# Input projection of a hybrid layer as seven products of 2x2 blocks, with its results taken through DRAM

## The chip, the cores and the metric

The kernel runs on one core of a Trainium2 chip. The metric is the device time of one execution in microseconds. The engines of the core are TensorE (PE in the profile; its weight loads are PEld), VectorE (DVE), ScalarE (ACT), GpSimd (POOL) and SyncE (SP), which issues nearly all DMAs of this kernel from one queue.

## What is computed

One layer of a decoder on 1024 prompt tokens and 64 sample tokens (8 sequences of 8), width 1024, float32: an FFN, a token mixing, a second FFN, and a final norm. The mixing projects each normed token to 8224 columns, and mixes by two branches:

```python
proj = hn @ w_in                                  # 1024 -> 1024 u, 2048 z, 3072 xbc, 32 dt, 2 x 1024 gates
branch_pool = pool_mix(u_ext, ...) @ pool_w_out   # trailing means over 2, 4, 8, 16 tokens, minus the token
xbc_c = silu(depthwise causal conv of width 4 over xbc)
dt = softplus(dt_raw + dt_bias)
y, new_ssm = ssd_scan(xs, dt, A, bm, cm, ssm_h0)  # Mamba-2 scan in chunks of 128 tokens, 32 heads in 4 groups
y = (y + d_skip * xs) * silu(z)                   # then an RMSNorm within each of the 4 groups
branch_ssd = y @ ssd_w_out
merged = sigmoid(g0) * branch_pool + sigmoid(g1) * branch_ssd
x = x + merged @ w_o
```

The last rows of u and xbc and the scan's states are outputs as well.

## The kernel before

**Layout.** Activations lie with channels on the 128 partitions and tokens along the free dimension. The tokens are worked on in two halves: half 0 has 512 prompt tokens, half 1 the other 512 and the 64 sample tokens, 576 in all. Matmul operands are kept as a high and a low part (F32R), and a product of two such operands is three matmuls: `products` (L274) issues high x high, high x low, low x high. `load_w` (L261) brings 4 blocks of 128 x 128 weights (256 KB), and ScalarE (L270) and VectorE (L271) split them into `wh` and `wl`. `dense` (L285) makes a tile of 128 output columns from 1024 input rows: 8 blocks x 3 matmuls of 512 columns for half 0, and twice as many of 288 for half 1.

**Seven products.** The FFNs make their first product for both halves at once by `wino` (L441): the matrix of weights is taken as 2x2 blocks of 512 rows x 128 columns, the tokens of a half as two quarters of 256 or 288, and seven products with sums of blocks replace eight. `wino_weights` (L402) forms the sums of weights on GpSimd (L411) and splits them (L417, L418); `combine` (L459) forms the sums of the operands on GpSimd (L472) and splits them (L478, L479); the results are added up when they leave PSUM. While `combine` works, the first tiles of an FFN are made by the plain form.

**The order.** The program is written out in full by Python, and its order decides what each engine finds next. Work that goes on beside the large products is a generator, a "chain" (`start`, `later`); `pe[0]` counts the TensorE time written so far, each chain says in how many microseconds of it the next step is due, and `tick`, called after each block of products, lets due chains write their step. `finish` writes all the rest of one chain at once. The pool of DMAs on SP's queue follows the same order.

**The mixing stage, half by half** (`mix_half`, L1260). It makes dt (`mix_dt`, L769), then u tile by tile with its trailing means, the group maps, the gates of the first branch and `pool_w_out` (`mix_pool`, L853), whose merged result goes to DRAM (`accd`). Then the four groups of the scan follow: `proj_group` (L985) makes a group's 6 conv tiles (`conv_tile`, L955: product, copy, four taps on ScalarE and VectorE, a tanh and a last product for SiLU). While the products of the next group and the z tiles (`z_tiles`, L1266) are written, the chain `ssd_group` (L1208) does the scan of the present one: for each chunk `ssd_a` (L1059) loads the broadcast decay rows (`ab`), transposes x, forms the masked decays and the operands; `ssd_b` (L1119) makes y and `ssd_st` (L1187) the next state. The y products (L1175 to L1180) use a zero-padded operand `xdtp`, 128 columns for two heads of 64, so that two matmuls add up into one block. For half 1 a fifth step per group does the sample tokens with their own states from DRAM. `gating` (L1240) multiplies by z, takes the group's norm (`rstd`, L325: squares, a column sum on TensorE, Newton steps on VectorE, a round trip through DRAM to spread the result over the partitions) and splits; then `ssd_out` (L1277) makes the group's part of `ssd_w_out`. In the last group the tiles of the second gate (`gate1`, L1288) are written, four of them between the scan and the wait for the last norm; then come the merge (`merge_head`, L1320) and `w_o`. Half 1 is normed (`norm_split`, L366) while half 0 is in `w_o`.

`N_ACT = 58` buffers of 128 x 576 are shared by most tiles of the stage.

Of the kernel before, what the change touches and what calls it, by code (L numbers as in the profile page):

```python
# [14 lines left out]
P = 128  # L15
# [22 lines left out]
N_FX, N_S, N_PDF = 17, 4, 6  # L38
N_PLAIN, N_APART = 3, 1
# [5 lines left out]
CONV_D = (1.0, 3.0)  # L45
# [12 lines left out]
N_PRE = 3  # L58


@with_exitstack
def tile_hybrid_pool_ssd_macaron(
# [42 lines left out]
    def fx(dt=F32, name="x"):  # L105
        if stage["name"] == "mix":
            return act((P, 576), dt, name)
        return stage["p"].tile([P, 576], dt, tag="fx", bufs=N_FX, name=nm(name))
# [101 lines left out]
    cwh = cp.tile([P, 5, 24], F32, tag="cwh", name="cwh")  # L210
# [10 lines left out]
    xdt_n = [0]  # L221
# [4 lines left out]
    def load_consts():  # L226
# [17 lines left out]
        for j in range(4):  # L244
            V.tensor_scalar_mul(cwh[:, j, :], cols[:, i_cw[j] : i_cw[j] + 24], 0.5)
        V.tensor_scalar_mul(cwh[:, 4, :], cols[:, i_cb : i_cb + 24], 0.5)
# [5 lines left out]
    accd = [[dp.tile([P, NTOK[h]], F32, tag=f"ac{h}_{m}", name=f"accd{h}_{m}") for m in range(KD)] for h in HALVES]  # L252
    acs_d = [dp.tile([4, NH, CH], F32, tag=f"acsd{h}", name=f"acsd{h}") for h in HALVES]
# [71 lines left out]
    def rstd(tiles, h, count, out, pace=1.0):  # L325
# [3 lines left out]
        s = act((P, N), name="ssq")  # L329
        for i, x in enumerate(tiles):  # L330
            if i == 0:
                S.activation(s, x, AF.Square)
            else:
                q = act((P, N), name="sq")
                S.activation(q, x, AF.Square)
                V.tensor_tensor(s, s, q, op=ALU.add)
            if i % 2:
                yield pace
# [26 lines left out]

    def norm_split(xt, h, gi, out, pace=1.0):  # L366

        N = NTOK[h]
        rr = []
        yield from rstd(xt, h, D, rr, pace)  # L370
        hi, lo = [], []
        for k in range(KD):
            a = act((P, N), F32R, "hi")
            b = act((P, N), F32R, "lo")
            t = act((P, N), name="xn")
            V.tensor_tensor(t, xt[k], rr[0], op=ALU.mult)
            split(t, a, b, cols[:, gi + k : gi + k + 1])
            hi.append(a)
            lo.append(b)
            yield pace  # L380
        out.append((h, hi, lo))

    def scaled(out, pts, h, r):

        for pt, (a, b) in zip(pts, PIECES[h]):
            V.tensor_tensor(out[:, a:b], pt[:, : b - a], r[:, a:b], op=ALU.mult)
# [162 lines left out]
    def ffn(wi, wo, prep, after, half=None):  # L549

        X, todo, behind = [{}, {}], [], []
        for h in HALVES:
# [10 lines left out]
            c = start(first(gen), T_AT[h + (2 if half else 0)])  # L565
            for ff in range(N_PLAIN):
                ffn_in_plain(wi, ff, x[:3])
            todo.append(c)
            behind.append(start(rest(c, gen)))
        for c in behind:  # L570
            finish(c)
        for ff in range(N_PLAIN, NFF - N_APART):
            ffn_in(wi, ff, [(h, X[h]) for h in HALVES])
# [3 lines left out]
        for h in HALVES:  # L577
# [12 lines left out]
            for ms in ((0, 1),) + tuple((m,) for m in range(2, KD)):  # L590
# [8 lines left out]
                for m, pts in zip(ms, po):  # L599
# [4 lines left out]
                    xt.append(x_)  # L604
                if half and ms[-1] == KD // 2 - 1:
                    half(h, xt)
# [87 lines left out]
    def norm_parts(xt, h, gi, out, pace=1.0):  # L694
# [3 lines left out]
        yield from rstd([t[:, :N] for t in xt], h, D, rr, pace)  # L698
        hi, lo, xn = [], [], []
        for k in range(KD):  # L700
            x = fx(name="xn") if k >= 4 else act((P, 576), name="xn")
            a, b = act((P, 576), F32R, "hi"), act((P, 576), F32R, "lo")
            V.scalar_tensor_tensor(x[:, :N], xt[k][:, :N], cols[:, gi + k : gi + k + 1], rr[0], op0=ALU.mult, op1=ALU.mult)
            split(x[:, :N], a[:, :N], b[:, :N])
            hi.append(a)
# [6 lines left out]
    ch, hn = {}, []  # L712
    wi1 = ffn1_w_in[0]

    def after1(h, xt):
        if h == 0:
            ch["hn"] = start(norm_split([t[:, : NTOK[0]] for t in xt], 0, i_gm, hn, HN_PACE))
        for m in range(KD):
            dma(xspill[h][m], xt[m][:, : NTOK[h]])
# [17 lines left out]
    ffn(wi1, ffn1_w_out[0], prep1, after1)  # L737
    finish(ch["hn"])
# [4 lines left out]
    xdtp = [stage["p"].tile([P, 4, 2, P], F32, tag=f"xdtp{i}", bufs=1, name=f"xdtp{i}") for i in range(2)]  # L743
    for t in xdtp:
        G.memset(t, 0.0)
    W = w_in[0]
    uhist = cp.tile([P, KD, HIST], F32, tag="uhist", name="uhist")
    chist = cp.tile([P, 24, 3], F32, tag="chist", name="chist")
# [11 lines left out]
    def evac_raw(pts, h, raw, off, raws, offs):  # L760

        if h == 0:
            S.copy(raw[:, off : off + 512], pts[0][:, :512])
            return
        S.copy(raw[:, off : off + 288], pts[0][:, :288])  # L765
        S.copy(raw[:, off + 288 : off + 512], pts[1][:, :224])
        S.copy(raws[:, :, offs : offs + NT], pts[1][:, 224:288].rearrange("p (b t) -> p b t", t=NT))

    def mix_dt(h, xs, out):  # L769
# [4 lines left out]
        pd = dense(W, 0, KD, OFF_DT, xs, name="pdt")[0]  # L774
        dfm = act((NH, N), name="dfm")
        for pt, (a, b) in zip(pd, PIECES[h]):
            S.activation(dfm[:, a:b], pt[:NH, : b - a], AF.Identity, bias=dtb)

        def chain():
            yield 8  # L780
# [28 lines left out]
            yield 12  # L809
# [40 lines left out]

        return start(chain())

    def mix_pool(h, xs, sin):  # L853

        N = NTOK[h]
        if h == 1:
# [71 lines left out]
        for gi in range(4):  # L928
            u_tile(2 * gi)
            u_tile(2 * gi + 1)  # L930
            if gi:
                group(gi - 1)
# [564 lines left out]
```

## Time and profile before

| | |
|---|---|
| median of 3 runs | 3033.59 us (3032.02 to 3039.48) |
| the profiled execution, first to last instruction | 3038.7 us |
| mean granted TensorE clock | 0.991 |
| TensorE busy | 2948.8 us, 97% |
| VectorE busy | 1747.2 us, 57% |
| ScalarE busy | 1263.1 us, 42% |
| GpSimd busy | 408.0 us, 13% |
| moved by DMA | 352.09 MB, 116 GB/s on average |

The page gives no time for the profiled execution beside its span. Durations below come from it alone. "Busy" of an engine is the time in which at least one of its instructions runs; matmuls are pipelined and their ends are modelled, so what one costs is read from start to start.

### The profile page before, as it was taken

To read this page: it belongs to the slowest core of one execution; us is meant where nothing else is said; L and a number is where in the kernel's file an instruction comes from. 1 tells how busy PE (TensorE), PEld (TensorE's weight loads), DVE (VectorE), ACT (ScalarE), POOL (GpSimd) and SP (SyncE) were. 2 spreads that over 40 slices of the span, in tenths; PEclk is the share of its full clock that TensorE was granted. 3 is DMA by queue.
4 is the path that set the end of the run, shared out by engine and by line. 5 is a ranking of instruction groups with operands and counts; after the bars stand their busy time and mean duration, and the time that the engine had idled before them with its cause. 6 is when DMAs were issued, how large, how long until landed. Compare 5 with 4: busy or idle time off the path is not lost. (4 is left out here: it accounts for less than half of the span.)

```text
span 3038.7 us, 51391 instructions
## 1 busy us (share of the span) xinstructions
PE 2948.8 (97%) x19636; PEld 2746.9 (90%) x19636; DVE 1747.2 (57%) x3456; ACT 1263.1 (42%) x2552; POOL 408.0 (13%) x491
## 2 busy tenths in 40 slices
PE   6999999999999999999999999999998999999998
PEld 5999999789988888878999989999988999997898
DVE  5544345434364897777725886968776433344442
ACT  5343334433243665434424554543344333343332
POOL 4333333000000000000001110100014333330000
PEclk9999999999999999999999999999999999999999
DMA  4443223653334333345333334244452222225552
GB/s 127 143 126 99 72 79 106 219 165 114 103 101 121 108 105 101 101 122 174 97 102 100 111 104 128 89 138 125 130 159 85 86 71 79 76 92 174 162 168 72
DMA packets 519273, 352.09 MB, mean 116 GB/s; under 512 B 27162, under 2 KB 460432, under 8 KB 519018
## 3 DMA queue, kind: packets, MB, share of 16 engines
q1 hardware_dynamic: 519010, 348.80, 38.4%
q8 instruction: 154, 2.52, 0.3%
q14 instruction: 93, 0.76, 0.1%
q10 hardware_dynamic: 16, 0.00, 0.0%
HBM read 291.65 MB, written 57.29 MB: 115 GB/s over the span
## 5 line engine op out<-in xcount | busy, mean ns | idle before, releaser
L270 ACT ACTIVATE wh<-wraw 128x512 fp32r<-128x512 f32 (+1 forms) x636 | 391.2, 619 | 806.2 <-PE po L160 257.7
L271 DVE TENSOR_TENSOR wl<-wraw,wh 128x512 fp32r<-128x512 f32 (+1 forms) x636 | 436.2, 688 | 494.3 <-ACT wh L270 466.7
L160 PE MATMUL pw<-hi,wh 128*128 128x288 f32 (+1 forms) x1216 | 351.7, 289 | 2.6 <-DVE t L522 2.2
L160 PE MATMUL pw<-hi,wl 128*128 128x288 f32 (+1 forms) x1216 | 350.8, 288 | 0.0
L160 PE MATMUL pw<-lo,wh 128*128 128x288 f32 (+1 forms) x1216 | 350.5, 288 | 0.0
L160 PE MATMUL pw<-X,wh 128*128 128x288 f32 (+1 forms) x1824 | 347.3, 289 | 1.1 <-ACT t L518 1.1
L160 PE MATMUL po<-hh,wh 128*128 128x288 f32 (+1 forms) x1056 | 289.7, 332 | 11.1 <-ACT hh L308 10.1
L160 PE MATMUL po<-hr,wh 128*128 128x288 f32 (+1 forms) x1056 | 290.3, 330 | 0.5 <-DVE hr L310 0.2
L160 PE MATMUL po<-hh,wl 128*128 128x288 f32 (+1 forms) x1056 | 289.8, 329 | 0.0
L160 PEld LDWEIGHTS pw<-X,wh 128*128 128x128 f32 x1824 | 288.1, 190 | 1.4 <-ACT t L518 1.4
L160 PE MATMUL pw<-X,wl 128*128 128x288 f32 (+1 forms) x912 | 263.0, 288 | 0.0
L160 PEld LDWEIGHTS pw<-hi,wh 128*128 128x128 f32 x1216 | 230.2, 189 | 3.5 <-DVE t L522 2.6
L160 PEld LDWEIGHTS pw<-lo,wh 128*128 128x128 f32 x1216 | 230.2, 189 | 0.0
L160 PEld LDWEIGHTS pw<-hi,wl 128*128 128x128 f32 x1216 | 230.1, 189 | 0.0
L418 DVE TENSOR_TENSOR wl<-s,wh 128x512 fp32r<-128x512 f32 x160 | 114.0, 714 | 175.3 <-ACT wh L417 172.5
L160 PEld LDWEIGHTS po<-hh,wh 128*128 128x128 f32 x1056 | 179.8, 190 | 30.2 <-ACT hh L308 15.3
L160 PEld LDWEIGHTS po<-hr,wh 128*128 128x128 f32 x1056 | 181.0, 190 | 17.5 <-DVE hr L310 3.9
L160 PEld LDWEIGHTS po<-hh,wl 128*128 128x128 f32 x1056 | 181.0, 190 | 14.6 <-DVE wl L271 0.7
L417 ACT ACTIVATE wh<-s 128x512 fp32r<-128x512 f32 x160 | 101.1, 632 | 181.4 <-PE pw L160 180.1
L160 PEld LDWEIGHTS pw<-X,wl 128*128 128x128 f32 x912 | 173.6, 190 | 0.0
L160 PE MATMUL pc<-hi,wh 128*128 128x288 f32 (+1 forms) x576 | 162.3, 335 | 0.7 <-ACT craw L765 0.6
L160 PE MATMUL pc<-hi,wl 128*128 128x288 f32 (+1 forms) x576 | 159.8, 329 | 0.3 <-DVE wl L271 0.3
(345 smaller groups left out, 6470.0 us busy)
## 6 DMA issues: line engine op xcount, KB each, us to landing
wraw<-in_w_in_dram SPq DMA_DIRECT2D x260, 256.0 KB
wraw<-in_ffn_w_in_dram SPq DMA_DIRECT2D x208, 256.0 KB
wraw<-in_ffn_w_out_dram SPq DMA_DIRECT2D x160, 256.0 KB
ab<-acsd SPq DMA_DIRECT2D x64, 256.0 KB
wraw<-in_ssd_w_out_dram SPq DMA_DIRECT2D x64, 256.0 KB
hd<-g SPq DMA_DIRECT2D x44, 288.0 KB
hr<-hd SPq DMA_DIRECT2D x44, 288.0 KB
hd<-g SPq DMA_DIRECT2D x44, 256.0 KB
```

The lines of the kernel that those rows point to most:

```text
L160: T.matmul(out, lhsT, rhs, start=start, stop=stop, skip_group_check=free)
L270: S.activation(wh, raw, AF.Copy)
L271: V.tensor_tensor(wl, raw, wh.bitcast(F32), op=ALU.subtract)
L417: S.activation(wh, a, AF.Copy)
L418: V.tensor_tensor(wl, a, wh.bitcast(F32), op=ALU.subtract)
```

## The change

**A projection stage of its own.** After the first FFN, still with its buffers and its 6 + 2 PSUM banks, all of the projection is made for both halves. dt and the first four z tiles are made plainly, half by half (`plain_in`), while the operands are combined; the other 60 tiles are made in pairs by `wino` (`proj_pair`). The trailing means and the convolution follow as chains on VectorE and ScalarE. SiLU is now one ScalarE function, where tanh and a product stood. All results go to DRAM: `convd`, `zd`, `gd`, `ddd`, `dtd_`. The squares for the norm between are taken as the FFN's tiles are finished (`squares`), and the normed half 0 is kept in DRAM (`xnd`) until it is combined.

**The mixing stage** loads these half by half. The scan of all 8 units (2 halves x 4 groups) is one chain, which may run `AHEAD = 2` groups in front of `ssd_out`. `mix_pool` of both halves stands first, then `mix_out` of half 0 and of half 1, each with `ssd_out` group by group, the merge and `w_o`.

**The y products** lose their zero padding: each head's 64 columns go to their own 64 partitions of the result. Four kinds of operation move from VectorE to GpSimd: the product with z, the last sum of y, the decay of the state, and one sum of the merge.

```diff
-N_FX, N_S, N_PDF = 17, 4, 6
-N_PLAIN, N_APART = 3, 1
+N_FX, N_S, N_PDF = 16, 4, 6
+N_PLAIN, N_APART, N_ZP = 3, 1, 4
...
+    def proj_pair(ca, cb, off, done, halves=HALVES, weights=None):
+        xs = [(h, XM[h]) for h in halves]
+        tiles = {}
+
+        def after(p, i, bk):
...
+            if p == "1":
+                S.copy(rb[:, l], A)
+            elif p == "2":
+                V.tensor_tensor(ra[:, f], B, rb[:, l], op=ALU.add)
+            elif p == "6":
+                S.copy(rb[:, f], A)
+            elif p == "5":
+                S.copy(rb[:, l], C)
+            elif p == "7":
+                V.tensor_tensor(rb[:, l], A, rb[:, l], op=ALU.add)
+            elif p == "3":
+                V.tensor_tensor(ra[:, l], C, rb[:, f], op=ALU.add)
+            else:
+                S.copy(rb[:, f], A)
+                done(h, ra, rb)
+
+        wino(wino_weights(W, 0, 4, 4, ca, cb), 4, xs, after)
...
+    def whole(f, scale, da, db):
+        def done(h, ra, rb):
+            for t, d in ((ra, da), (rb, db)):
+                S.activation(t[:, : NTOK[h]], t[:, : NTOK[h]], f, scale=scale)
+                dma(d[:, slice(*TOK[h])], t[:, : NTOK[h]])
...
+    finish(prepm[0][0])
+    prepm[0][1][0] = prepm[0][1][0][:3] + (xn0,)
+    XM = operands(prepm, plain_in, M_AT)
...
+    for k in range(0, KD, 2):
+        u_pair(k, sin, ost)
+        if zs:
+            z_pair(zs.pop(0))
+    settle()
+    pool_out_rows(ost)
+    for g in range(NG):
+        hist, st_, c = conv_in(g)
+        finish(c)
+        conv_pair(16 + g, 20 + g, hist, st_, 0)
+        if zs:
+            z_pair(zs.pop(0))
+        conv_pair(4 * g, 4 * g + 1, hist, st_, 2)
+        conv_pair(4 * g + 2, 4 * g + 3, hist, st_, 4)
+        gate_pair(4 * g)
+        settle()
+        conv_out(g, st_)
+    for j in (2, 6, 10):
+        gate_pair(j)
+    for h in HALVES:
+        gate_pair(14, (h,))
...
+    def load_group(h, g):
...
+        dma(Bf, convd[16 + g][:, hs])
+        dma(Cf, convd[20 + g][:, hs])
+        for j in range(4):
+            dma(xs4[:, j, :N], convd[4 * g + j][:, hs])
...
-            mm(py[:, (i // 2) * L : (i // 2 + 1) * L], xp[:L, i // 2, i % 2, :], m_, start=(i % 2 == 0), stop=(i % 2 == 1))
+            mm(py[(i % 2) * HD : (i % 2 + 1) * HD, (i // 2) * L : (i // 2 + 1) * L], xp[:L, i * HD : (i + 1) * HD], m_)
...
-            V.tensor_tensor(ysl, ysl, ea, op=ALU.add)
+            G.tensor_tensor(ysl, ysl, ea, op=ALU.add)
...
-                V.tensor_tensor(hn_.rearrange("p (h d) -> p h d", d=HD), hold.rearrange("p (h d) -> p h d", d=HD),
+                G.tensor_tensor(hn_.rearrange("p (h d) -> p h d", d=HD), hold.rearrange("p (h d) -> p h d", d=HD),
...
-            V.scalar_tensor_tensor(y4[:, j, :N], z4[j], 0.5, y4[:, j, :N], op0=ALU.mult, op1=ALU.mult)
+            G.tensor_tensor(y4[:, j, :N], z4[j], y4[:, j, :N], op=ALU.mult)
+            squares(sums, y4[:, j, :N])
...
+    def until(ready):
+        while not ready():
+            min(chains, key=lambda q: q.due).step()
+
+    def scan():
+        units = [(h, g) for h in HALVES for g in range(NG)]
+        nxt = load_group(*units[0])
+        for u, (h, g) in enumerate(units):
+            N, hs = NTOK[h], slice(*TOK[h])
+            cur = nxt
+            while u - used[0] > AHEAD:
+                yield 1.0
+            while not dts[h]:
+                yield 1.0
+            y4 = big(name="y4")
+            body = ssd_group(h, g, *cur, y4, dts[h])
+            yield next(body)
+            if u + 1 < len(units):
+                nxt = load_group(*units[u + 1])
+            z4 = []
+            for w in body:
...
+                yield w
+            yn = []
+            pend[h, g] = (start(gating(h, g, y4, z4, yn)), yn)
...
+        def yn(g):
+            until(lambda: (h, g) in pend)
+            finish(pend[h, g][0])
+            used[0] += 1
+            return pend.pop((h, g))[1][0]
...
-                V.tensor_tensor(acc2[m], acc2[m], ac, op=ALU.add)
+                G.tensor_tensor(acc2[m], acc2[m], ac, op=ALU.add)
...
-    c, _ = mix_half(0, hn[0], prep_b)
-    finish(c)
-    c, x1 = mix_half(1, hb[0], prep_a2)
+    cdt = mix_dt(0, dts[0])
+    start(scan())
+    mix_pool(0)
+    mix_dt(1, dts[1])
+    mix_pool(1)
+    mix_out(0, lambda: None, None)
+    c, x1 = mix_out(1, prep_a2, sums2)
```

More of the change, by code (lines that the diff above doesn't have):

```diff
@@ L252, in tile_hybrid_pool_ssd_macaron, with rows_of @@
     accd = [[dp.tile([P, NTOK[h]], F32, tag=f"ac{h}_{m}", name=f"accd{h}_{m}") for m in range(KD)] for h in HALVES]
+    TOK = ((0, 512), (512, 1088))
+    def rows_of(name, n, w=NTOK[0] + NTOK[1], p=P):
+        return [dp.tile([p, w], F32, tag=f"{name}{k}", name=f"{name}{k}") for k in range(n)]
+    xnd = rows_of("xnd", KD, NTOK[0])
+    convd, zd, ddd, gd = (rows_of(a, b) for a, b in (("cv", 24), ("zd", 16), ("dd", KD), ("gd", 16)))
+    dtd_ = rows_of("dtr", 1, p=NH)[0]
     acs_d = [dp.tile([4, NH, CH], F32, tag=f"acsd{h}", name=f"acsd{h}") for h in HALVES]
@@ L323, in newton, with squares, rstd @@
             V.scalar_tensor_tensor(r, t, 1.5, r, op0=ALU.add, op1=ALU.mult)
-    def rstd(tiles, h, count, out, pace=1.0):
+    def squares(s, x):
+        N = x.free_size()
+        if not s:
+            s.append(act((P, N), name="ssq"))
+            S.activation(s[0], x, AF.Square)
+        else:
+            q = act((P, N), name="sq")
+            S.activation(q, x, AF.Square)
+            V.tensor_tensor(s[0], s[0], q, op=ALU.add)
+    def rstd(tiles, h, count, out, pace=1.0, sums=None):
         N = NTOK[h]
         nch = 4 + h
[L329 to L338, printed above, removed]
+        if sums is None:
+            sums = []
+            for i, x in enumerate(tiles):
+                squares(sums, x)
+                if i % 2:
+                    yield pace
+        s = sums[0]
         yield max(pace, 1.5)
@@ L547, in ffn_in_plain, with operands @@
         dma(hdram[h][ff], g[:, : NTOK[h]])
-    def ffn(wi, wo, prep, after, half=None):
-        X, todo, behind = [{}, {}], [], []
+    def operands(prep, plain, at):
+        X, behind = [{}, {}], []
         for h in HALVES:
@@ L563, in first @@
                     yield p
[L565 to L568, printed above, removed]
+            c = start(first(gen), at[h])
+            plain(x[:3])
             behind.append(start(rest(c, gen)))
@@ L571, in ffn, with plain @@
             finish(c)
+        return X
+    def ffn(wi, wo, prep, after, half=None, sums=None):
+        def plain(x):
+            for ff in range(N_PLAIN):
+                ffn_in_plain(wi, ff, x)
+        X = operands(prep, plain, T_AT[2:] if half else T_AT[:2])
         for ff in range(N_PLAIN, NFF - N_APART):
@@ new lines, in plain_in @@
+    def plain_in(x):
+        h, N = x[0], NTOK[x[0]]
+        pd = dense(W, 0, KD, OFF_DT, [x], name="pdt")[0]
+        d = fx(name="dfm")[:NH]
+        for pt, (a, b) in zip(pd, PIECES[h]):
+            S.activation(d[:, a:b], pt[:NH, : b - a], AF.Identity, bias=dtb)
+        dma(dtd_[:, slice(*TOK[h])], d[:, :N])
+        for j in range(N_ZP):
+            pz = dense(W, 0, KD, OFF_Z + j * P, [x], name="pz")[0]
+            z = fx(name="z")
+            func(z, pz, h, AF.Silu)
+            dma(zd[j][:, slice(*TOK[h])], z[:, :N])
@@ L758, in reload, with mix_dt @@
         return t
[L760 to L769, printed above, removed]
+    def mix_dt(h, out):
         N = NTOK[h]
```

484 lines of the change are left out of this document (224 added, 260 removed).

## The prediction

> **What bounds the kernel now.** First the page's table of engines, then windows of the trace laid over the stages.
>
> ```profile
> span 3038.7 us, 51391 instructions
> PE 2948.8 (97%) x19636; PEld 2746.9 (90%) x19636; DVE 1747.2 (57%) x3456; ACT 1263.1 (42%) x2552; POOL 408.0 (13%) x491
> ```
>
> TensorE is at work for 97% of the span, so what removes TensorE time shows in the end, and what leaves TensorE without work is paid in full. The mixing stage runs from its first matmul, into pdt, to its last, into pwo:
>
> ```profile
> L160 PE MATMUL pdt<-hi,wh x24: 290/298/467, 813.2 to 1442.3; 128*128 128x288 f32 x16, 128*128 128x512 f32 x8
> L160 PE MATMUL pwo<-mh,wh x192: 292/302/442, 1389.6 to 2251.2; 128*128 128x288 f32 x128, 128*128 128x512 f32 x64
> ```
>
> That is 813.2 to about 2252, 1439 us; its second half begins at 1442. The windows (us, then busy time of PE, PEld, DVE, ACT, POOL with instruction counts, granted clock, DMA share, GB/s):
>
> ```profile
> 300.00:400.00 100.00, 100.00 (x797) 100.00 (x796) 38.80 (x70) 38.49 (x82) 32.47 (x28) 1.00 0.25 77
> 813.00:1442.00 629.00, 622.61 (x2974) 515.10 (x2974) 457.89 (x886) 296.39 (x534) 11.85 (x62) 1.00 0.40 116
> 1442.00:2252.00 810.00, 797.18 (x5936) 775.51 (x5936) 575.31 (x1298) 363.02 (x777) 48.76 (x103) 0.99 0.41 117
> 1000.00:1100.00 100.00, 99.79 (x501) 82.64 (x500) 89.96 (x181) 61.07 (x114) 3.92 (x20) 1.00 0.40 114
> 1800.00:1900.00 100.00, 93.99 (x691) 90.04 (x690) 71.80 (x165) 49.47 (x108) 2.81 (x8) 0.97 0.39 113
> 2200.00:2300.00 100.00, 89.93 (x519) 80.93 (x517) 73.22 (x123) 43.39 (x81) 28.38 (x28) 0.93 0.46 144
> ```
>
> The first row is the seven-product form in the first FFN: TensorE never idles and VectorE is under 40%. The mixing stage is TensorE-bound too, but VectorE is busy for 458 + 575 = 1033 of its 1439 us, and in 1000 to 1100 it reaches 90% while TensorE still has 99.8%. The change takes TensorE work out of this stage and leaves nearly all the scan's VectorE work, with less beside it: that balance decides. DMA moves 117 GB/s at a share of 0.41, so it does not bound here.
>
> **The change part by part.** *The projection.* Start times of the matmuls give what one really costs (the listed 0.28 to 0.39 us overlap):
>
> ```profile
> 299.88 0.28 PE L160 MATMUL pw<-hi,wh 128*128 128x256 f32 x1
> 301.30 0.30 PE L160 MATMUL pw<-hi,wh 128*128 128x288 f32 x1
> 302.89 0.28 PE L160 MATMUL pw<-hi,wh 128*128 128x256 f32 x1
> 969.89 0.39 PE L160 MATMUL pc<-hi,wh 128*128 128x512 f32 x1
> 975.33 0.39 PE L160 MATMUL pc<-hi,wh 128*128 128x512 f32 x1
> wraw<-in_w_in_dram SPq DMA_DIRECT2D x260, 256.0 KB
> ```
>
> Twelve matmuls of 256 columns take 1.42 us (0.118 each), twelve of 288 take 1.59 (0.1325), and 24 of 512 take 5.44 (0.227). A 128-column tile of the projection is now 24 of 512 for the first half and 48 of 288 for the second: 5.44 + 6.36 = 11.80 us. There are 65 (260 loads, two per tile and half): 767 us. Afterwards dt and four z tiles stay plain, 5 x 11.80 = 59 us, and 60 tiles make 30 pairs of 7 x 12 = 84 matmuls for each half: 9.94 + 11.13 = 21.07 us a pair, 632 in all. 767 - 691 = **-76 us**. It is 10%, not an eighth: a matmul of 256 or 288 costs more per column than one of 512. The row of 300 to 400 shows this form without a hole, and its sums on POOL, splits and evacuations are the same code, so I cost them at nothing; conv and pooling arithmetic lies beside it, where VectorE has 60 us in 100 free. If that cover failed, a conv pair's twelve 0.75 us products would show beside 21 us of TensorE.
>
> *Stalls that do not come back.* Part of the projection is now threaded between scan steps, and 1800 to 1900 shows 6 us lost in 100. Between 0 and 25 us over the stage; I take **-12**.
>
> *What is left for the scan to hide behind.* The dense products left are:
>
> ```profile
> wraw<-in_ssd_w_out_dram SPq DMA_DIRECT2D x64, 256.0 KB
> wraw<-in_pool_w_out_dram SPq DMA_DIRECT2D x32, 256.0 KB
> wraw<-in_w_o_dram SPq DMA_DIRECT2D x32, 256.0 KB
> wraw<-in_pool_w_group_dram SPq DMA_DIRECT2D x8, 256.0 KB
> ```
>
> 136 loads, 68 a half, each 12 matmuls of 512 (2.72 us) or 24 of 288 (3.18): 401 us. 1439 - 767 - 401 leaves 271 us for the scan's own matmuls, sums and transposes, with their stalls. With TensorE full the new mixing stage would last 401 + 271 = 672 us, and the change gains as long as that stage stays under 748. VectorE's work in it: from the 1033 us, what leaves or moves.
>
> ```profile
> L271 DVE TENSOR_TENSOR wl<-wraw,wh 128x512 fp32r<-128x512 f32 (+1 forms) x636 | 436.2, 688 | 494.3 <-ACT wh L270 466.7
> L979 DVE SCALAR_TENSOR_TENSOR ct<-craw,cwh,ct x144: 734/747/757, 969.2 to 1950.3; 128x512 f32<-128x512 f32 x144
> L979 DVE SCALAR_TENSOR_TENSOR ct<-crs,cwh,ct x72: 270/278/290, 1624.3 to 1950.9; 128x64 f32<-128x64 f32 x72
> L982 DVE SCALAR_TENSOR_TENSOR xs<-cth,ct x32: 681/720/771, 983.6 to 1952.0; 128x512 f32<-128x512 f32 x16, 128x576 f32<-128x576 f32 x16
> L1273 DVE SCALAR_TENSOR_TENSOR z<-z,pz x48: 445/448/683, 1039.7 to 2141.6; 128x288 f32<-128x288 f32 x32, 128x512 f32<-128x512 f32 x16
> L895 DVE TENSOR_TENSOR us<-us x24: 684/699/706, 843.2 to 1509.4; 128x524 f32<-128x524 f32 x12, 128x520 f32<-128x520 f32 x8, 128x512 f32<-128x512 f32 x4
> L1185 DVE TENSOR_TENSOR y<-y,ea x32: 419/686/693, 1050.9 to 2124.6; 128x512 f32<-128x512 f32 x28, 128x256 f32<-128x256 f32 x4
> L1202 DVE TENSOR_TENSOR hst<-hst,cd x28: 676/684/692, 1037.2 to 2076.4; 128x512 f32<-128x512 f32 x28
> L1244 DVE SCALAR_TENSOR_TENSOR y<-z,y x32: 684/722/759, 1067.0 to 2142.1; 128x512 f32<-128x512 f32 x16, 128x576 f32<-128x576 f32 x16
> L1327 DVE TENSOR_TENSOR acc<-acc,ac x16: 684/722/758, 1343.1 to 2173.4; 128x512 f32<-128x512 f32 x8, 128x576 f32<-128x576 f32 x8
> ```
>
> 260 weight splits at 0.688 (179), conv 144 x 0.747 + 72 x 0.278 (128), its last product for 48 tiles at 0.72 (35), z 32 x 0.447 + 16 x 0.683 (25), pooling sums 40 x 0.70 (28) leave the stage; the four last rows, 21 + 19 + 23 + 12 = 75 us, go to POOL. 1033 - 470 = 563 us stay, 84% of 672.
>
> *The moved work meets VectorE on its way.* 108 operations go to POOL. The same shape there costs about twice as much, and the two engines hold each other up when both read two operands from SBUF:
>
> ```profile
> L411 POOL TENSOR_TENSOR s<-wraw,wraw 128x512 f32<-128x512 f32 x80 | 104.6, 1308 | 218.9 <-DVE wl L418 163.2 <-DMA wraw<-in_ffn_w_in_dram 53.1 <-DMA hd<-g 2.5
> L479 DVE TENSOR_TENSOR X<-xn,X x32: 411/654/1636, 40.7 to 2318.5; 128x256 fp32r<-128x256 f32 x16, 128x288 fp32r<-128x288 f32 x16
> L472 POOL TENSOR_TENSOR xn<-xn x16: 724/1116/1272, 25.7 to 2285.0; 128x256 f32<-128x256 f32 x8, 128x288 f32<-128x288 f32 x8
> ```
>
> L479 and L472 run beside each other, and one form takes 411 ns or 1636, 724 or 1272. Per POOL operation VectorE may lose nothing or half of 1.3 us; I take 0.3, so 32 us, and 595 us of VectorE. The last 86 us of the stage (below) hold little of it, some 35 us; 560 us fall into the other 586. At the 90% of the window of 1000 to 1100 they need 622, so up to 36 us are exposed; that window lost nothing at 90%, so the low end is zero. Small pooling and norm rows that leave as well are still in my 563, so I take two thirds: **+24**. By the Trainium skill, page "SBUF — State Buffer", section "Who interferes with whom", the engines share an exclusive lock, and whoever comes second waits the whole instruction; L479 agrees with it.
>
> *The end of the stage.* The last group's norm, in order of time:
>
> ```profile
> 2142.08 0.76 DVE L1244 SCALAR_TENSOR_TENSOR y<-z,y 128x576 f32<-128x576 f32 x1
> L308 ACT ACTIVATE yh<-y,cols x4: 776/778/780, 2160.7 to 2169.5; 128x576 fp32r<-128x576 f32 x4
> ```
>
> From the last product to the first operand of ssd_w_out are 18.6 us, with a round trip through DRAM in them. Now four gate tiles (gate1, 4 x 6.36 = 25 us) stand beside them. Afterwards those are long done, nothing dense is left but what waits for this norm: behind it in TensorE's queue stand the last eight pso tiles and w_o (8 + 16 loads x 3.18 = 76 us, with the transposes and norm sums some 86). At least 19 us, at most 40 if the last sample steps stand bare too; **+24**.
>
> *The two entries.* The projection now needs the second half's norm and both halves' operands right after the first FFN, as ffn2 does; 2200 to 2300 shows such an entry: 10 us idle, clock 0.93. Bounds 0 and 20, **+10**. The new mixing stage begins with loads of what was just stored, behind the last gate stores on SP's queue: 0 to 10, **+5**. Later loads (convd, zd, gd, ddd: 64 tiles, written and read once, about 70 MB) replace half the 260 projection loads (34 MB); 117 GB/s x 1439 us + 37 MB are 205 MB over some 1400 us, 146 GB/s, what 2200 to 2300 moves at a share of 0.46, so I cost them at nothing; if that cover failed, each group's six loads would stand ahead of its scan. *Clock:* the same row gives 0.93 where 10 us idled, 813 to 1442 gives 1.00 where 6 did; for some 60 us of new idle I take **+5** (0 to 20).
>
> *No zero padding.* The eight y products of a chunk:
>
> ```profile
> 1063.60 1.95 PE L160 MATMUL pyd<-ab,xdtp 128*128 128x128 f32 x16
> 1065.30 0.48 PE L160 MATMUL pc<-hi,wh 128*128 128x512 f32 x1
> ```
>
> 16 records from 1063.60 to 1065.30, 1.70 us; 32 chunks, 54 us. The number and the moving columns stay. If the 64-wide products cost what they do now, 0; if two run at once, -27; a change of shape could cost a little. **-8**, near the row, since TensorE is not always the last here. By the Trainium skill, page "TensorEngine Tiling (Array Packing)", section "Key Properties", different tiles can run in parallel, but a change of tiling mode drains TensorE; by its first half this term would be -27, by its second above zero, and no row here shows either.
>
> Sum: -76 - 12 + 24 + 24 + 10 + 5 + 5 - 8 = **-28 us**. The profiled execution has a span of 3038.7, 5 us above the median of the runs, 3033.6; I take the difference off the median: **3006 us**.
>
> **The rivals.**
> 1. *Cover holds.* TensorE stays full as in 1000 to 1100 (middle 0), most interleaving stalls vanish (-25), y costs half (-27), entries 5: -76 - 25 - 27 + 24 + 5 = -99, 2935 us. For: 90% VectorE beside 99.8% TensorE exists. Against: it must last 600 us, not 100.
> 2. *The lock in full.* Each of 108 POOL operations holds VectorE for 0.65 us: 70 us, VectorE 633, the middle at 90% needs 664 against 586, 78 exposed instead of 24: 3060 us. For: L479's 1636. Against: the FFN window, where both work and TensorE has no hole.
> 3. *The norm's wait at every group (slower).* ssd_out of each group waits for that group's norm, and the projection that stood in front of it is gone. If the next unit's scan does not fill TensorE there, six more waits of up to 18.6 us, 112 instead of 24: -28 + 88 = +60, 3094 us. It decides from 52/6 = 9 us of bare wait per group. For: a group's ssd_out is only 8 loads, 22 to 25 us, and the planner wants to spread a group's scan over nine steps of 4.8 to 6.5 us. Against: the scan may run two groups ahead, and a group's scan has some 34 us (271/8) of TensorE work of its own.
> 4. *Only moved.* 60 of 65 tiles change form and the entries and waits eat all 76 us: about 3034.
>
> **How the numbers follow.** This kernel's measurement tells 0.3% (9 us) from no change. Forecast (2975 to 3024) 0.44; rival 1 (below 2975) 0.20; rival 4 (3024 to 3043) 0.08; rival 2 0.12; rival 3 0.16. Faster 0.44 + 0.20 = 0.64, same 0.08, slower 0.28. The likeliest case's own range is 2975 to 3024. The range takes in nearly all of rival 1 and rival 2, and leaves out the tail of rival 3: 2930 to 3080.
>
> **What would show it.** The projection as one stretch of about 700 us at the row of 300 to 400, 84 matmuls a pair and half; else the -76 is wrong. The mixing stage of about 730 us with VectorE near 90%: 675 is rival 1. POOL at 20% there, and two-operand VectorE rows far above 0.69 us, are rival 2. Idle TensorE before each pso, released by yh or yl, is rival 3. pyd records under 0.1 us apart show the padding's gain. I am wrong if DMA waits lead the list of waits.

## The result, and the profile after

The changed kernel takes **3245.03 us** (median of four runs, 3243.45 to 3246.82), against 3033.11 of the kernel before (3032.02 to 3039.48): ratio **1.0693, 95% interval 1.0678 to 1.0708**. The prediction was 3006 us, a little faster; the kernel is 212 us slower than the one before, and above the upper end of the range.

The profile page of the changed kernel first: span, the table of engines, and the granted clock in 40 slices.

```profile
span 3243.4 us, 53826 instructions
PE 2930.0 (90%) x20356; PEld 2752.0 (85%) x20356; DVE 1787.8 (55%) x3404; ACT 1307.3 (40%) x2645; POOL 761.0 (23%) x785
PEclk9999999999999999999989879876788999999999
```

TensorE went from 97% of the span to 90%, and in nine of the 40 slices its clock is below 9 tenths. Which slices these are is seen from the first and last matmuls of the stages: pdt starts at 829.5 (before: 813.2), the first grouped pooling product, pgm, at 1562.2, and the last pwo ends at 2454.4. The windows over the projection and the mixing stage, and a stretch of 100 us in each (us, busy time of PE, PEld, DVE, ACT, POOL with instruction counts, granted clock, DMA share, GB/s):

```profile
829.50:1562.00 732.50, 711.39 (x5477) 701.14 (x5475) 469.52 (x806) 362.24 (x738) 266.18 (x340) 0.99 0.35 108
1562.00:2455.00 893.00, 687.89 (x4154) 597.04 (x4154) 600.88 (x1326) 338.79 (x661) 147.66 (x118) 0.83 0.47 145
1100.00:1200.00 100.00, 100.00 (x797) 99.96 (x796) 66.82 (x117) 55.62 (x111) 37.12 (x53) 1.00 0.36 111
2200.00:2300.00 100.00, 72.70 (x459) 65.87 (x457) 66.31 (x156) 31.43 (x62) 21.18 (x16) 0.72 0.49 152
```

The projection in its steady part (1100 to 1200) is as foretold: TensorE has no hole, with VectorE at 67%. The mixing stage lasts 893 us, and in them TensorE is at work for 688, at a clock of 0.83. VectorE is busy for only 67% of it: nothing is full there. Set beside the prediction's own parts (profiled executions, us; 701 is its 691 + 10, and 710 its 672 - 12 + 24 + 24 + 5 + 5 - 8):

| stretch | predicted | measured | off by |
|---|---|---|---|
| up to the first pdt | 813 | 829.5 | +16 |
| projection | 701 | 733 | +32 |
| mixing stage | 710 | 892 | +182 |
| behind it (second FFN) | 787 | 789 | +2 |

What does TensorE wait for in the mixing stage? The list of its waits there (waiting instruction, releaser, us in total, times, longest):

```profile
PE pss L163 <- DVE ssq L340: 55.6, 8, 9.7
PE pso L163 <- ACT yh L314: 34.3, 6, 6.6
PE pgm L163 <- ACT dh L314: 15.4, 4, 5.8
PE prt L167 <- DVE rsm L329: 14.7, 6, 2.9
PE px L167 <- ACT xr L1149: 13.0, 3, 8.2
PE pst L163 <- DVE xd L1210: 12.0, 1, 12.0
PE pwo L163 <- DVE x L1455: 11.2, 4, 4.1
```

In the kernel before, the same list over the whole of its stage (813 to 2252) begins with 2.8 us:

```profile
PE pso L160 <- ACT acc L1284: 2.8, 2, 1.5
PE pso L160 <- DVE wl L271: 2.6, 3, 1.5
PE pso L160 <- ACT yh L308: 2.1, 1, 2.1
```

pss, prt and pso are three links of one chain, a group's gated norm: 55.6 + 14.7 + 34.3 = 105 us. One of them in order of time (start us, duration, engine, line, operation; in brackets the idle time ahead and its releaser):

```profile
2228.36 1.11 PE L167 MATMUL pfin<-ident,hst 128*128 128x128 f32 x4
...
2230.34 5.98 POOL L1351 TENSOR_TENSOR y<-z,y 128x576 f32<-128x576 f32 x4
...
2238.51 2.17 PE L163 MATMUL pss<-ones,ssq 128*128 128x1 f32 x10 [9.03 <-DVE ssq L340]
...
2243.06 0.38 PE L167 MATMUL prt<-ident,rsm 128*5 128x128 f32 x1 [2.38 <-DVE rsm L329]
...
2244.99 0.35 SPq L375 DMA_DIRECT2D r<-rd  x1
...
2249.01 2.10 DVE L1359 TENSOR_TENSOR y<-y,r 128x576 f32<-128x576 f32 x3 [3.75 <-DMA r<-rd]
2249.80 2.11 ACT L314 ACTIVATE yh<-y,cols 128x576 fp32r<-128x576 f32 x3 [4.25 <-DVE y L1359]
2250.63 1.33 PE L163 MATMUL pso<-yh,wh 128*128 128x288 f32 x4 [5.70 <-ACT yh L314]
```

The group's scan ends at 2229; the gate's products on GpSimd, the squares, the sum over partitions, the Newton steps, the trip through DRAM and the first split follow each other, and ssd_out starts at 2250.6. In 21.5 us TensorE does 4.4 us of work. pss waits in this way at 1776, 1843, 1922, 2043, 2138 and 2345 too, seven times in all, and at all but the first prt and pso follow.

The waits cost more than they last. Matmuls that follow the last of them (the x2 rows are pairs of one shape):

```profile
2254.45 0.68 PE L163 MATMUL pso<-yh,wh 128*128 128x288 f32 x2
2254.94 0.68 PE L163 MATMUL pso<-yl,wh 128*128 128x288 f32 x2
2255.41 0.49 PE L163 MATMUL pso<-yh,wl 128*128 128x288 f32 x2
2255.75 0.42 PE L163 MATMUL pso<-yh,wh 128*128 128x288 f32 x2
2256.01 0.43 PE L163 MATMUL pso<-yl,wh 128*128 128x288 f32 x2
```

Two matmuls of 288 columns take 0.49 us from 2254.45, and 0.26 from 2255.75. The windows show the clock that goes with it:

```profile
2204.40:2229.10 24.70, 24.67 (x120) 23.18 (x120) 10.57 (x35) 4.48 (x8) 0.59 (x1) 0.50 0.44 124
2229.10:2250.60 21.50, 4.41 (x20) 3.54 (x18) 8.47 (x21) 4.63 (x9) 8.22 (x6) 0.50 0.27 85
2250.60:2255.40 4.80, 4.77 (x18) 4.49 (x19) 4.69 (x7) 2.09 (x3) 0.00 (x0) 0.50 0.53 196
2255.60:2260.40 4.80, 4.80 (x38) 4.80 (x37) 3.39 (x11) 3.18 (x7) 0.00 (x0) 1.00 0.00 0
```

18 matmuls in 4.8 us, then 38: TensorE runs at half its clock through the hole and for another 4.9 us after it. The first row shows that the hole did not start this: in the 24.7 us before it, where the sample tokens' small products follow each other with no hole over 0.8 us, the granted clock is 0.50 too. The same holds at the waits of 2138 and 2345: the half clock begins at 2115.6 and 2323.8, some 12 us ahead of the hole and in sample steps too. At the waits of 1843, 1922 and 2043 it begins inside the hole. By the Trainium skill, page "TensorE: Matmul & The Clock Gate", section "Part 1: The HAM clock gate", throttled is the default state, and about 3.4 us of sustained activity release it. This trace agrees about the half clock, and its 4.9 us are somewhat more; the 24.7 us of small products at half clock do not fit the 3.4 us.

From the start times of all matmuls, each held against the usual interval of its shape, the mixing stage splits into some 570 to 580 us of matmuls at their usual intervals, 214 us in 53 holes of over 0.8 us, and 103 to 114 us of smaller excess, depending on what is taken as usual; much of it is intervals about twice the usual one (0.24 us for 0.13 at 288 columns). The kernel before has 16 us in 11 holes and 60 to 67 us of small excess in its whole stage.

### The profile page after: what moved, and what is told of

It reads as the page before. It is cut to its first block, busy times and chain, and to the rows that moved or that the text cites. A ratio compares the mean times of both kernels' runs of the same rounds, so it can differ in the third digit from the quotient of the medians.

```text
span 3243.4 us, 53826 instructions
## 1 busy us (share of the span) xinstructions
PE 2930.0 (90%) x20356; PEld 2752.0 (85%) x20356; DVE 1787.8 (55%) x3404; ACT 1307.3 (40%) x2645; POOL 761.0 (23%) x785
## 5 line engine op out<-in xcount | busy, mean ns | idle before, releaser
L163 PE MATMUL pw<-hi,wh 128*128 128x288 f32 (+1 forms) x2176 | 630.3, 290 | 3.6 <-DVE t L514 2.1
L163 PE MATMUL pw<-hi,wl 128*128 128x288 f32 (+1 forms) x2176 | 628.5, 289 | 1.4 <-DVE wl L410 1.4
L163 PE MATMUL pw<-lo,wh 128*128 128x288 f32 (+1 forms) x2176 | 627.9, 289 | 0.0
L163 PE MATMUL pw<-X,wh 128*128 128x256 f32 (+1 forms) x3264 | 625.0, 290 | 0.4 <-ACT rb L763 0.4
L163 PEld LDWEIGHTS pw<-X,wh 128*128 128x128 f32 x3264 | 518.5, 191 | 0.9 <-ACT rb L763 0.7
L163 PE MATMUL pw<-X,wl 128*128 128x256 f32 (+1 forms) x1632 | 472.8, 290 | 0.1
L163 PEld LDWEIGHTS pw<-hi,wh 128*128 128x128 f32 x2176 | 412.4, 190 | 4.7 <-DVE t L514 2.5
L163 PEld LDWEIGHTS pw<-hi,wl 128*128 128x128 f32 x2176 | 412.2, 189 | 1.8 <-DVE wl L410 1.8
L163 PEld LDWEIGHTS pw<-lo,wh 128*128 128x128 f32 x2176 | 412.4, 190 | 0.0
L403 POOL TENSOR_TENSOR s<-wraw,wraw 128x512 f32<-128x512 f32 x142 | 192.8, 1357 | 424.5 <-DVE wl L410 314.6
```

Source lines behind the costliest of these rows:

```text
L163: T.matmul(out, lhsT, rhs, start=start, stop=stop, skip_group_check=free)
L403: G.tensor_tensor(t, a, b, op=op)
```

## The experiments

Three theories for the 182 us. **W**: each group's norm stands bare in front of its ssd_out, since the dense work that used to stand there is gone (the prediction's rival 3). **L**: the operations that went to GpSimd, by the lock or by their length. **C**: the scan's VectorE work no longer fits beside what TensorE has left (the prediction's "middle"). "Stage" is the mixing stage from the first pgm to the end of the last pwo in the profiled execution; ratios are to the kernel before on the same chip.

| run | time us | ratio, interval | stage us |
|---|---|---|---|
| the change | 3245.03 | 1.0693, 1.0678 to 1.0708 | 892 |
| nonorm | 3201.38 | 1.0539, 1.0509 to 1.0570 | 845 |
| thread | 3220.89 | 1.0604, 1.0573 to 1.0634 | 866 |
| lag | 3180.71 | 1.0471, 1.0431 to 1.0511 | 832 |
| vback | 3239.78 | 1.0666, 1.0635 to 1.0697 | 879 |
| fill | 3259.5 | 1.0733, 1.0717 to 1.0749 | 899 |
| spread | 3237.74 | 1.0675, 1.0658 to 1.0692 | 882 |
| lag2 | 3154.45 | 1.0405, 1.0385 to 1.0425 | 808 |
| lagspread | 3165.05 | 1.0446, 1.0424 to 1.0469 | 817 |
| lagnn | 3143.3 | 1.0372, 1.0346 to 1.0398 | 789 |
| nosq | 3221.93 | 1.0632, 1.0609 to 1.0654 | 890 |
| best | 3135.97 | 1.0320, 1.0299 to 1.0341 | 804 |
| bestvb | 3136.48 | 1.0326, 1.0301 to 1.0351 | 804 |
| beststep | 3121.7 | 1.0268, 1.0244 to 1.0292 | 789 |
| ypad | 3017.42 | 0.9940, 0.9927 to 0.9954 | |

**nonorm: the norm's factor off the path.**

```diff
-        yield from rstd(None, h, 512, rr, GP[0], sums)
+        start(rstd(None, h, 512, [], GP[0], sums))
...
-            V.tensor_tensor(y4[:, j, :N], y4[:, j, :N], rr[0], op=ALU.mult)
```

> The changed kernel, but a scan group's result goes to ssd_out without the group's norm factor: the sums, Newton steps and the round trip through DRAM are still done, as a chain of their own that nothing waits for. Left out: the product with the norm factor (32 VectorE products, 22 us). Theory W (the norm of each group, written as one piece ahead of ssd_out, stands bare before TensorE): the waits at pss, prt and yh fall from about 18 us a group to some 8 (product with z and split remain), so 8 x 10 us and with them part of the lowered clock: 80 to 140 us faster than the changed kernel. Theory L (work moved to GpSimd holds VectorE up): no more than the 22 us of products. Theory C (the scan's VectorE work simply does not fit beside the products left): about 22 us as well.

It gave 44 us (1.0693 to 1.0539), half of what W expected at least, twice what the others did. pss and prt leave the head of the list of waits, but pso takes over:

```profile
PE pso L163 <- ACT yh L314: 48.6, 6, 9.5
```

So the factor is only a part of the bare chain: the gate's products on GpSimd and the splits remain in front of pso.

**thread and lag: the order.** In thread, ssd_out waits for its own norm alone, and scan steps that come due are written in between. In lag it also waits until the next group's scan is written out.

```diff
-            finish(pend[h, g][0])
+            until(lambda: pend[h, g][0].done)          # thread
+            c = h * NG + g                             # lag
+            until(lambda: pend[h, g][0].done and (c == 7 or divmod(c + 1, NG) in pend))   # lag
...
         while not ready():
-            min(chains, key=lambda q: q.due).step()
+            c = min(chains, key=lambda q: q.due)
+            pe[0] = max(pe[0], c.due)
+            c.step()
```

> As lag, but ssd_out waits only for its own group's norm: the norm is written in its due steps, with two or three steps of the next scan between them, where the changed kernel writes it in one piece. W: some 5 to 10 us of matmuls go into each of 7 waits, 30 to 70 us faster than the changed kernel, less than lag. L and C: within 15 us.

> The changed kernel, but ssd_out of a group is written only once the scan of the next group is written, and while chains are forced the planner's clock moves on to the step that is due, so that a group's norm is written among the next group's scan. Nothing is left out. W: TensorE has the next scan's matmuls (17 to 35 us) in front of it while the norm runs; of 7 waits of 18 us most goes, 70 to 130 us faster than the changed kernel, and the wait of the last group stays. L and C: within 20 us of the changed kernel, since the work of each engine is the same.

-24 and -64 us by the medians. Nothing is computed otherwise, only the order in which the steps are written differs, so the order is a cause. Both fall a little short of W's sizes (30 to 70 and 70 to 130); in lag 19 us on pss and 21 on pso are left.

**vback: GpSimd's part.** The four operations go back to VectorE (G. to V. in four lines).

> The changed kernel with its four kinds of GpSimd operation (product with z, last sum of y, decay of the state, one sum of the merge) back on VectorE, as they are before the change. L: VectorE's two-operand products are no longer held up and the stage gets 50 us or more shorter. W: the chain before each norm loses about 3 us (four products at 0.75 instead of 1.5 us), VectorE gains 75 us of work in a stage where it idles a third of the time: between 25 us faster and 15 slower than the changed kernel. C: some 50 us slower.

5 us by the medians, with intervals that overlap: L falls, and so does C, which gave some 50 us more. The window over its mixing stage, columns as above:

```profile
1566.00:2445.00 879.00, 690.81 (x4154) 599.41 (x4154) 629.87 (x1433) 338.56 (x662) 4.34 (x10) 0.83 0.48 147
```

VectorE does 107 operations more than in the changed kernel (1433 for 1326) and is busy 29 us longer (630 for 601). The summed durations of the operations that both kernels have on VectorE are 34 us shorter in vback: 0.31 us lost on VectorE for each of the 108 operations on GpSimd. The loss is there, at the size that the prediction took for the lock, and costs next to nothing in the end.

**fill: is it the clock?** Products of the identity by itself fill TensorE's queue ahead of the norm's three waits.

```diff
+            T.matmul(pt[:, 384:512], ident, ident, start=True, stop=True)   # 32, 8 and 20 times
```

> The changed kernel, with products of the identity by itself (results never read) put into TensorE's queue in front of the three matmuls of a group's norm that wait: 32 ahead of pss, 8 ahead of prt, 20 ahead of the first pso. The order of everything else is as it was. Theory K (the low granted clock of the mixing stage, 0.83, comes from TensorE's own holes, and costs some 77 us beyond what the waits last): the clock in the mixing stage rises to 0.9 or more, the small excess over the usual matmul interval falls from 103 us to 50 to 75, and the time falls by 20 to 50 us against the changed kernel. Rival D (the clock follows something else, such as the work of the other engines or DMA, or the waits hide what the clock costs): the clock stays at 0.80 to 0.86 and the time within 10 us, or rises by the filler that does not fit, up to 30 us.

+12 us by the ratios: K's gain did not come, and D had allowed for as much by filler that does not fit. The mean clock of the stage rose to 0.89, between what the two gave, but the filler's own matmuls count in it. The small excess stayed where it was, which goes against K, and the holes went from 214 to 117 us for 106 us of filler. One of the seven waits shows why:

```profile
2260.91 4.18 PE L347 MATMUL pfl<-ident 128*128 128x128 f32 x36
...
2268.16 0.79 PE L163 MATMUL pso<-yh,wh 128*128 128x288 f32 x4 [2.29 <-ACT yh L314]
2269.42 0.85 PE L163 MATMUL pso<-yl,wh 128*128 128x288 f32 x2 [0.47 <-DVE yl L318]
```

A hole of 2.3 us is left behind the filler, and from 2269.4 to 2272.5 the matmuls run at 0.24 us again. A filler that leaves a hole buys no clock here. Whether one that leaves none would pay was not tried, and what the half clock costs by itself is not separated from the holes.

**spread and lagspread: the place of the dense work.** The second half's pooling branch moves behind the first half's outputs, alone and together with lag2 (below).

```diff
-    mix_pool(1)
     mix_out(0, lambda: None, None)
+    mix_pool(1)
```

> The changed kernel with the pooling branch of the second half put after the first half's ssd_out and w_o instead of before them. Nothing is left out. Theory W (what is missing is dense work beside the scan: both pooling branches, about 200 us, stand in front, where the scan may run only two groups ahead): the second branch now covers two groups of the second half, two bare norm chains and part of the scan's own waits vanish, -20 to -60 us against the changed kernel. Rival L/C (the place of the dense work does not matter, VectorE's sum or the chain inside the scan decides): within 12 us.

> The run with ssd_out one group later and the norm's steps further apart (3154 us), and with the second half's pooling branch behind the first half's outputs. Theory W (cover): with the norm away from the path, the second branch covers scan steps of the second half that now stand bare, and the 90% window of VectorE at 1860 to 1960 is spread out: 3115 to 3140 us. Rival S (VectorE or the scan's own chain is what is left, and the place of the dense work does not count, as in the run that moved it alone, -5 us): 3146 to 3165.

-7 us by the medians (the intervals overlap), and with lag2 +11: my theory of the place fell twice. The 200 us of dense work cover about as much in one place as in the other while the same waits are written in the same order.

**lag2 and lagnn: the norm further off the path.** lag2 is lag with the norm's steps written further apart; lagnn also takes the factor out, as nonorm does.

```diff
-        yield max(pace, 1.5)
+        yield 9.0 if count == 512 else max(pace, 1.5)
...
-        yield R_WAIT0
+        yield R_WAIT0 + (4.0 if count == 512 else 0.0)
...
-        yield R_WAIT
+        yield R_WAIT + (5.0 if count == 512 else 0.0)
```

> As the run with ssd_out one group later (3181 us), and the steps of the group norm written further apart: 9 us of TensorE work ahead of pss instead of 1.5, 4 more ahead of prt, 5 more behind the reload. Theory W: the 19 us on pss and 7 on prt that were left in that run go, and 10 of the 22 us on pso: mixing stage 805 to 820 instead of 838, 3150 to 3165 us. Rival S (the scan's own chain sets the rate once the norm is away; a later norm only delays the buffers): within 8 us of 3181, with px, pcb, pst and pyd in front of the list of waits.

> The run with ssd_out one group later and the norm's steps further apart (3154 us), and the group norm's factor computed beside the path and not multiplied in (left out: 32 products on VectorE, as in the run without the norm's wait). Theory W says that the norm's wait is wholly gone in 3154 already: within 12 us of it, less the 16 us or so that the 32 products take on VectorE where it is the last; 3135 to 3158 us. Rival N (a good part of the norm chain still stands on the path): below 3130 us, with no pss, prt or pso among the first waits.

lag2 takes 91 us off the changed kernel by the medians (87 by the ratios), within what W gave. lagnn differs from it by 11 us, less than its 32 left-out products are on VectorE, so the norm's factor costs at most that in lag2. Its list of waits still has 35 us on links of the chain (pss 2.7, prt 7.3, pso 16.1 on yh and 8.6 on yl), where the changed kernel had 105. This settles the first cause: **the group norm's chain, written in one piece in front of ssd_out, costs some 90 us with the half clock around it.**

**nosq: the first FFN.** The squares of the norm that follows the first FFN are taken in the norm again, and the spill behind it.

```diff
-    ffn(wi1, ffn1_w_out[0], prep1, after1, sums=sums1)
+    ffn(wi1, ffn1_w_out[0], prep1, after1)
...
-        prepm.append((start(norm_parts(xt, h, i_gm, o, HN_PACE, "place" if h else "dram", sums1[h])), o))
+        prepm.append((start(norm_parts(xt, h, i_gm, o, HN_PACE, "place" if h else "dram")), o))
+        for m in range(KD):
+            dma(xspill[h][m], xt[m][:, : NTOK[h]])
```

> The changed kernel with one part undone: the squares of the first norm are not taken tile by tile behind the first FFN's out product, but together in the norm, as before; the spill follows them. Nothing is left out. Theory F (the 16 us by which the projection starts late come from act buffers that the inline squares and sums hold, so that the loads of hh come late): the first pdt at 813 to 820 instead of 829.5, the waits of po for hh back to 11 us; the projection's entry 3 to 6 us longer, since the second half's squares now stand there; in all -5 to -12 us. Rival: the later loads come from the new norm's other tiles or N_FX 16: pdt at 827 or later, in all 0 to +8 us.

-23 us (-19 by the ratios), more than expected. pdt starts at 811.5. In the other runs that leave the first FFN as it is in the changed kernel, it starts between 828.8 and 835.2. The changed kernel's waits from 600 to its pdt had one row that nosq lacks:

```profile
PE po L163 <- ACT hh L314: 10.7, 8, 2.3
```

The rest of the expectation did not come: the projection is not longer (728 us for 733). That the squares, their sums and the earlier spill delay the loads of hh is shown; that it is by act buffers is argued, since the run moved buffers and stores together.

**best, bestvb, beststep: what is left.** best is lag2 and nosq together; bestvb also puts the four operations back on VectorE; beststep writes the scan's steps closer together (STEP 4.0 and 3.0 for 6.5 and 4.8, STEP_S 1.6 for 2.5).

> The changed kernel with ssd_out one group later, the norm's steps further apart, and the first norm's squares taken in the norm again. Nothing is left out. If the two causes (the group norm's chain in front of ssd_out, -91 us; the inline squares in the first FFN, -23 us) are separate, they add: 3245 - 91 - 23 = 3131, between 3122 and 3142 us. If the second only moves the work to a place where the first hides it: 3148 or more.

> The run before in this call, with the four operations that went to GpSimd back on VectorE (about 100 of them, some 75 us of VectorE's time in the mixing stage). Theory V (with the norm away VectorE is what the rest waits for: it had 82 to 91% in 1760 to 1960): 20 to 60 us slower than the run beside it. Rival H (the rest is many short waits of TensorE on chains of several engines and the half clock behind them, no engine's sum): within 12 us of it, or faster, since VectorE does these operations in half GpSimd's time.

> The first run of this call with the scan's steps written closer together (4.0 and 3.0 us of TensorE work between them instead of 6.5 and 4.8, 1.6 instead of 2.5 for the sample steps). Theory V: VectorE is full, so nothing is gained, within 10 us. Theory P (the dense work in front, two pooling branches, is used up before the scan has got as far as it could): the scan gets through more of itself beside the pooling branches, -15 to -40 us. Rival H (each step then has less work between it and what it waits for): 10 to 40 us slower.

The two causes add (3136 for the 3131 expected). The windows over the mixing stage, of best:

```profile
1543.00:2348.00 805.00, 675.91 (x4154) 575.69 (x4154) 610.70 (x1326) 338.12 (x662) 163.07 (x118) 0.90 0.52 161
```

and of bestvb:

```profile
1540.00:2345.00 805.00, 671.07 (x4154) 572.36 (x4154) 620.31 (x1434) 338.11 (x660) 4.45 (x10) 0.90 0.52 161
```

The same time, as rival H had it. The test is weaker than I meant it: the 108 operations add only 10 us to VectorE's busy time, because the others get shorter when GpSimd does not work beside them (the splits of weights alone by 21 us, 115 to 94), so V could show in 10 us at most, not in 75. With vback (29 us more on VectorE, no time lost) and VectorE at 76% of the stage in best, nothing is left that speaks for VectorE's sum as the bound. In the waits of best in its mixing stage no single chain stands out any more:

```profile
PE pgm L163 <- ACT dh L314: 15.3, 4, 5.8
PE pso L163 <- ACT yh L314: 15.3, 5, 8.1
PE pwo L163 <- DVE x L1460: 11.7, 4, 4.2
PE pcb L163 <- DVE ea L1291: 10.2, 6, 3.8
PE pst L163 <- DVE xd L1212: 8.0, 6, 3.1
```

pss, prt and pso on yh and yl come to 33 us. 47 holes, 132 us, and small excess as large as in the changed kernel: many short waits of TensorE on chains of several engines, and the clock behind them; that these make up the rest is read from the list, not shown by a run. beststep takes 14 us off (16 by the ratios), about the lower end of theory P. How much of the last 80 to 90 us of the stage another order would take away stays open.

**ypad: one part alone, on the kernel before.** The y products without zero padding.

```diff
-        V.tensor_tensor(xpo, pxv, dtv, op=ALU.mult)
+        V.tensor_tensor(xp[:L, :].rearrange("p (h d) -> p h d", d=HD), px[:L, :].rearrange("p (h d) -> p h d", d=HD),
+                        dt[:L, hcs].unsqueeze(2).broadcast_to([L, HPG, HD]), op=ALU.mult)
...
-            mm(py[:, (i // 2) * L : (i // 2 + 1) * L], xp[:L, i // 2, i % 2, :], m_, start=(i % 2 == 0), stop=(i % 2 == 1))
+            mm(py[(i % 2) * HD : (i % 2 + 1) * HD, (i // 2) * L : (i // 2 + 1) * L], xp[:L, i * HD : (i + 1) * HD], m_)
```

> The kernel before with one part of the change alone: the y products without zero padding (64-wide operands, two column tiles), the pair of padded tiles and their memset gone. The prediction took 8 us off for it (0 to 27). From the trace of the changed kernel, where the records of pyd stand 0.101 us apart instead of 0.112: 512 records, 5 to 6 us, so 3028 to 3033 where the kernel before takes 3034 to 3038. Rival: a change of the tile shape costs as much as it gives, within 2 us.

0.994 (0.9927 to 0.9954): **18 us faster**, by far more than expected. It is the only version that beats both kernels. Its TensorE timeline around one chunk:

```profile
1062.24 1.09 PE L160 MATMUL pyd<-ab,xp 128*64 128x128 f32 x16
1063.27 0.50 PE L160 MATMUL pc<-hi,wh 128*128 128x512 f32 x1
```

16 records in 1.03 us, where the prediction's rows have 1.70 for the padded form. The expectation's 0.101 us was misread: the records come in pairs, 0.007 and 0.100 us apart, so the mean interval is half of it.

## Why the prediction was wrong

**The -76 of the projection held.** At their usual intervals its matmuls take 696 us, where 691 were worked out, and 1100 to 1200 shows no hole. Of the 42 us above 691 (10 of them predicted), 22 are holes and 14 small excess: the split weights at the entry, and pust waiting for GpSimd's cst, 8 us in four waits, a helper that was costed at nothing. The split of these by runs was not tried.

**The step that failed is "The end of the stage".** It took the last group's norm, saw that its four gate tiles of cover go, and charged 24 us once. The cover of the other groups goes in the same way. That was rival 3, set aside because "the scan may run two groups ahead, and a group's scan has some 34 us of TensorE work of its own". The scan is allowed to run ahead, but the code writes a group's whole norm in one piece in front of its ssd_out, and between prt and pso above TensorE has only five transposes and one small product (two records) of the next group:

```profile
2243.23 1.06 PE L167 MATMUL pxT<-ident,xs 128*128 128x128 f32 x4
2244.09 0.63 PE L163 MATMUL pcb<-Cf,Bf 128*128 128x128 f32 x2
2244.51 0.42 PE L167 MATMUL pcb<-ident,Bf 128*128 128x128 f32 x1
```

lag and lag2, which change nothing but that order, give back 64 and 91 us.

**Rival 3 itself was priced too low.** It said six more waits of up to 18.6 us, 88 us beyond the forecast's 24; its sum put their 112 in the place of the 24, where six more waits would add to it (3118, not 3094). The waits at the seven groups came to about 105 us, close to its 112, but the half clock around the holes was not in it (the prediction had +5 us for the clock, and the stage ran at 0.83), and other waits were not either: 214 us of holes in all, half of them outside the norm's chain. Some 37 us of these (27 before pgm, 10 before pbp) stand in the two pooling branches, the very work that was to cover the scan; the prediction's +5 for the entry is the only term near them, and no run was made on them.

**"The middle" had the wrong reason.** Its +24 came from VectorE's sum against the time that TensorE leaves. The sum was right: 595 us predicted, 601 measured, and the lock's 0.3 us for each of GpSimd's operations measured 0.31. But vback keeps VectorE busy for 29 us more and loses nothing, and in the slower kernel it is busy for only 67% of the stage. What dense work had been hiding was the length of the chains, not VectorE's sum; the 90% row of 1000 to 1100 showed an engine that could be that full with an unrelated matmul always at hand, and nothing about a stage without one. "VectorE near 90%", the sign for the forecast, did not come.

**A term that was missing.** +16 us in the first FFN, which the prediction left as it was: nosq.

**No zero padding was -8, and is about -18** where it stands alone. 1.70 to 1.03 us for each of 32 chunks would be 21. The 64-wide products run two at a time: their 16 records take 0.064 us each, where the padded ones stand 0.112 us apart. This agrees with the first half of what the prediction took from the Trainium skill, page "TensorEngine Tiling (Array Packing)", section "Key Properties", that different tiles can work in parallel. Its second half, that a change of mode drains TensorE, no run shows by itself; if the wider gap ahead of the first record is such a drain (0.205 us for 0.112), it is 0.09 us a chunk. The low bound of -27 was nearer than the value taken.

**DMA** was costed at nothing and did not lead: the two stages together moved 128 GB/s over 1626 us, 208 MB for the 205 foretold, and the mixing stage 145 GB/s at a share of 0.47; no DMA stands among TensorE's long waits.

## What to carry to other kernels

Dense work that is taken out of a stage was also the cover of every latency chain in that stage. Before the change, follow one round of each chain (scan, norm, output) through the timeline, and ask what stands between its links in TensorE's queue once the dense products are gone; do it for every group, not for the last alone, and price each hole with the half clock around it. Sums of busy time do not answer it: here the stage got 182 us longer than foretold while no engine was above 77%.

## What the runs showed that was not expected

- TensorE at half clock for 24.7 us of small products without a hole over 0.8 us (120 records, ahead of 2229), and for 4.9 us after a hole of 5.7 us (18 matmuls in 4.8 us, then 38); after a hole of 2.3 us that followed filler, a few matmuls at the usual interval and then 3.1 us at 0.24.
- The records of 64-wide fp32 products into the two halves of one PSUM tile stand in pairs, 0.007 us apart: eight products take 1.03 us where the zero-padded 128-wide form takes 1.70.
- 0.31 us of VectorE time lost for each of 108 two-operand operations moved to GpSimd (34 us in all), with a change of 5 us, within the intervals, in the kernel's time. Between best and bestvb it is 0.5 us each (56 us over 108).
